# Hybrid decoder layer on one core: other start addresses for the activation tiles, and wide-and-narrow matmul pairs in part of the program

## The chip, the cores and the metric

The kernel runs on one core of one Trainium2 chip. The metric is the device time of one launch, in microseconds (us); the median of three runs of the kernel before is 1642.35 us (1641.98 to 1642.44).

## What is computed

One decoder layer on 256 tokens of width 2048, in float32. An input projection (2048 to 13312 columns) feeds three branches: a gated linear recurrence with 8 heads, causal pooling, and a spatial gating unit. Each branch output of width 1024 is projected to 2048 and weighted by its own gate; the sum goes through an output projection and a layer norm. Then follows a gated feed-forward net with a causal depthwise convolution, and a second layer norm. Cut to what matters here:

```python
merged = (gates[:, :, 0] * (y_hg @ w_hg_proj[l])
          + gates[:, :, 1] * (y_pool @ w_pool_proj[l])
          + gates[:, :, 2] * (y_sg @ w_sg_proj[l]))
mix = merged @ w_out[l]
x = layer_norm(DN_ALPHA * x + mix, ln1_g[l], ln1_b[l])
h = x @ w_up                            # 2048 -> 2 * 5632
acc = conv_b + sum_j conv_w[j] * (h shifted by 2 - j tokens)
a, b = jnp.split(acc, 2, axis=-1)
x = layer_norm(DN_ALPHA * x + (silu(a) * b) @ w_down, ln2_g[l], ln2_b[l])
```

## The kernel before, in words

**Two-part operands.** Every float32 operand of the large products is split (`split`, line 71) into a high part, a rounded copy made by ScalarE, and a low part, the difference made by VectorE. A product is then three matmuls: high x high, high weights x low activations, low weights x high activations. An activation tile holds for each of its k-steps (128 rows of the contraction) 512 columns: 256 tokens of high parts and next to them 256 of low parts.

**Weights.** `pieces` (line 80) loads 1 MB at a time from HBM into `raw` (two buffers), on SP's queue, and splits it into `whi` and `wlo`, a ring of four buffers each, 4 KB a partition and piece. The tiles of `const`, `wst` and the later pools stand one behind the other in each partition; the sizes in front of the ring put every `whi` and `wlo` buffer at 128 modulo 256 bytes, before and after.

**Feature-major groups.** `feat_major` (line 114) computes 256 output features for all 256 tokens: the weights are the stationary operand (128x128) and the activations move, 256 columns at a time. `fm_piece` (line 103) goes k-step by k-step and for each of two column blocks issues the three matmuls of lines 110, 111 and 112, all into the same 256 columns of a PSUM bank. A group over 2048 rows is 16 k-steps, 96 matmuls. The input projection (moving tile X) runs so for its feature-major parts; the branch projections run so with moving tiles y (8 k-steps, 48 matmuls), and the up-projection with x1T. The accumulator tile `mm` (two banks) rotates through three buffers.

**Token-major groups.** `tok_major` (line 138) has the activations as weights and moves 512 columns of `whi` or `wlo`: lines 149 to 151. The value parts of the input projection and the output projection (stationary tile X, for the latter the merged tile that takes X's buffer), and the down-projection (stationary tiles aT).

**Order of the program.** Pool inputs and spatial-gating inputs, the recurrence's inputs, then three merge stages (`merge`, line 601: gate 1, gate 2, gate 0; each 8 times a gate group with X and a projection group with y, with the steps of the recurrence in between), the output projection, the first layer norm, whose transposed result is x1T (`x1T0` and `x1T1`, line 639), the up-projection (line 776: j from 0 to 21, two halves each, so 44 groups; the first has a code of its own, `feat_major_halves`, line 120), and the down-projection. The order on TensorE is as written; on the other engines a scheduler places the work, `hp()` asking for priority. In the up-projection ScalarE and VectorE apply the three taps of the convolution straight from the accumulator into `cv`; only the first group goes through a copy `fm_low` and a sum `h`.

**Where the tiles start.** X is allocated from the right end of the partition, 32768 bytes, and starts at 224 modulo 256. x1T0 and x1T1 come first in the pool `ff` and start at 128; the y tiles in `mix` start at 192; the aT tiles in `up` start at 128.

Of the kernel before, what the change touches and what calls it, by code (L numbers as in the profile page):

```python
# [8 lines left out]
F32 = mybir.dt.float32  # L9
F32R = mybir.dt.float32r  # L10
U8 = mybir.dt.uint8
AF = mybir.ActivationFunctionType
# [4 lines left out]
P = 128  # L17
S = 256
NT = S // P
D = 2048  # L20
KD = D // P
W = 1024
KW = W // P
DFF = 5632
KF = DFF // P
# [4 lines left out]
RMS_EPS = 1e-6  # L30
LEVELS = (64, 32, 16, 8, 4, 2, 1)
RAW_BUFS = 2
KEEP = 14
ENDS = (256, 512)
CROSS = 5
# [5 lines left out]
def hybrid_layer(  # L41
# [6 lines left out]
    nc = tc.nc  # L48
    ctx.enter_context(tc.manual_schedule(engines={ENG.PE}))
    x2 = x[0]  # L50
    win, wup, wout, wdown = w_in[0], w_up[0], w_out[0], w_down[0]

    def hp(level=1):
        return tc.high_priority(offset=1000000 * level)
# [4 lines left out]
    def add(o, a, b):  # L59
        nc.vector.tensor_tensor(out=o, in0=a, in1=b, op=ALU.add)  # L60

    def mul(o, a, b):
        nc.vector.tensor_tensor(out=o, in0=a, in1=b, op=ALU.mult)  # L63

    def stt(o, a, s, b, op0, op1):
        nc.vector.scalar_tensor_tensor(out=o, in0=a, scalar=s, in1=b, op0=op0, op1=op1)  # L66

    def act(o, a, f, **kw):
        nc.scalar.activation(out=o, in_=a, func=f, **kw)  # L69

    def split(hi, lo, src, low=nc.vector):
        act(hi, src, AF.Copy)
        low.tensor_tensor(out=lo, in0=src, in1=hi.bitcast(F32), op=ALU.subtract)  # L73
# [6 lines left out]
    def pieces(w2, col, width, kt_n, big, step, home=None, low=lambda k0: nc.vector):  # L80
        wv = w2.rearrange("(k p) c -> p k c", p=P)
        for b0 in range(0, kt_n, big):
            bn = min(big, kt_n - b0)
            with hp():
                raw = wst.tile([P, bn, width], F32, name="raw", bufs=RAW_BUFS)
                nc.sync.dma_start(out=raw, in_=wv[:, b0:b0 + bn, col:col + width])
            for s0 in range(0, bn, step):
                n = min(step, bn - s0)
                with hp():
                    hi, lo = (home or stage)(b0 + s0, n, width)  # L90
                    split(hi, lo, raw[:, s0:s0 + n, :], low(b0 + s0))
                yield b0 + s0, n, hi, lo

    def stage(k0, n, width):
        return (wst.tile([P, n, width], F32R, name="whi"), wst.tile([P, n, width], F32R, name="wlo"))

    def mm_tile():
        return ps_mm.tile([P, 2, 512], F32, name="mm")
# [1 line left out]
    def ax_tile():  # L100
        return ps_ax.tile([P, 512], F32, name="ax")

    def fm_piece(ps, xT, kt_n, k0, n, hi, lo):
        for k in range(n):
            kt = k0 + k
            for c in range(2):
                cs = slice(c * P, (c + 1) * P)
                xv = xT(kt)
                pc = ps[:, c, 0:S]
                nc.tensor.matmul(pc, lhsT=hi[:, k, cs], rhs=xv[:, 0:S], start=kt == 0, stop=False)  # L110
                nc.tensor.matmul(pc, lhsT=hi[:, k, cs], rhs=xv[:, S:2 * S], start=False, stop=False)  # L111
                nc.tensor.matmul(pc, lhsT=lo[:, k, cs], rhs=xv[:, 0:S], start=False, stop=kt == kt_n - 1)  # L112

    def feat_major(w2, col, xT, kt_n, big=8, step=4, ready=()):
        ps = mm_tile()
        for piece in ready or pieces(w2, col, 256, kt_n, big, step):
            fm_piece(ps, xT, kt_n, *piece)
        return ps[:, :, 0:S]

    def feat_major_halves(kept, xT, kt_n, between):  # L120
        ps = mm_tile()
# [16 lines left out]
    def tok_major(w2, col, xT, kt_n, big=4, step=2, last=0, home=None, done=None, during={}, ends=(512,)):  # L138
# [37 lines left out]
            c0 = c1  # L176
        return ps

    def bc(t, n):
        return t.rearrange("p (a b) -> p a b", b=n)  # L180

# [31 lines left out]

    xpool_cm = tc.tile_pool(name="xpool", bufs=1, side="right", reuse_waits="tile")
    xpool = xpool_cm.__enter__()
    xT_t = xpool.tile([P, KD, 2 * S], F32R, name="X")

    def xT(k):
        return xT_t[:, k, :]

    mix_cm = tc.tile_pool(name="mix", bufs=1, reuse_waits="tile")
    mix = mix_cm.__enter__()
# [10 lines left out]
    def fm_a():  # L233
        return mix.tile([P, 2, S], F32, name="fm_a", bufs=2)
# [11 lines left out]
    def first_block(col):  # L246
# [24 lines left out]
        for i in range(len(STARTS)):  # L271
            cur = nxt
            if i + 1 < len(STARTS):
                nxt = prepare(*STARTS[i + 1])
            else:
                early.extend(next(second) for _ in range(2))
            fm_piece(ps, xT, KD, *cur)
# [84 lines left out]
    for j in range(2):  # L362
        ps = tok_major(win, 6144 + 512 * j, xT, KD)
# [28 lines left out]
    def pool_out(g):  # L392
        ps = feat_major(pool_w[0, g], 0, lambda k: pooled[g][:, k, :], 2, step=2)
        with hp():
            for c in range(2):
                k = 2 * g + c
                scale = pscale[:, k:k + 1]
                hi = y_pool[:, k, 0:S]
                act(hi, ps[:, c, :], AF.Copy, scale=scale)
                stt(y_pool[:, k, S:2 * S], ps[:, c, :], scale, hi.bitcast(F32), ALU.mult, ALU.subtract)  # L400
# [15 lines left out]
    for j in range(4):  # L416
        ps = feat_major(win, 5120 + 256 * j, xT, KD)
# [183 lines left out]
    def merge(first, gi, y, wp, side=()):  # L601
        side = iter(side)
        gcol = 7168 + D * gi
        for j in range(8):
            ps = feat_major(win, gcol + 256 * j, xT, KD)
            gt = fm_a()
            with hp():
                act(gt, ps, AF.Sigmoid)
            next(side, None)
            ps = feat_major(wp, 256 * j, lambda k: y[:, k, :], KW)  # L610
            aj = acc[:, 2 * j:2 * j + 2, :]
            with hp():
                if first:
                    mul(aj, ps, gt)
                else:
                    mul(gt, ps, gt)
                    add(aj, aj, gt)
            next(side, None)
        for _ in side:
            pass  # L620
# [5 lines left out]
    merge(False, 2, y_sg, w_sg_proj[0], hgrn_steps(1, *hgrn(1), o_hg))  # L626
    split(y_hg[:, 4:8, 0:S], y_hg[:, 4:8, S:2 * S], o_hg[1])
    merge(False, 0, y_hg, w_hg_proj[0])
    mT_t = xpool.tile([P, KD, 2 * S], F32R, name="X")
    for j in range(8):  # L630
        split(mT_t[:, 2 * j:2 * j + 2, 0:S], mT_t[:, 2 * j:2 * j + 2, S:2 * S], acc[:, 2 * j:2 * j + 2, :])
    mix_cm.__exit__(None, None, None)
# [3 lines left out]

    ff_cm = tc.tile_pool(name="ff", bufs=1, reuse_waits="tile")
    ff = ff_cm.__enter__()
    x1T_h = [ff.tile([P, KD // 2, 2 * S], F32R, name=f"x1T{i}") for i in range(2)]
    x1 = ff.tile([P, NT, D], F32, name="x1")  # L640
    st1 = ff.tile([P, NT, 4, 6], F32, name="st1")
    for j in range(4):
        cs = slice(512 * j, 512 * (j + 1))
        nc.gpsimd.dma_start(out=x1[:, :, cs], in_=x2[:, cs].rearrange("(t p) c -> p t c", p=P))

    keep_cm = tc.tile_pool(name="keep", bufs=KEEP // 2, reuse_waits="tile")
    keep = keep_cm.__enter__()
# [5 lines left out]
    def keep_home(k0, n, width):  # L653
        if k0 < KD - KEEP:
            return stage(k0, n, width)
        return (keep.tile([P, n, width], F32R, name="khi"), keep.tile([P, n, width], F32R, name="klo"))
# [40 lines left out]
    for j in range(3):  # L697
        cs = slice(512 * j, 512 * (j + 1))
        ps = tok_major(wout, 512 * j, mT, KD)
# [6 lines left out]
    up_next = pieces(wup, DFF, 256, KD, 8, 4)  # L706
    up_early = []
# [26 lines left out]
    def wout_during(c):  # L734
        with hp(2):
            ln1_turn(0, c)
            if 0 < c < 3:
                ln1_low(0, c - 1)
            if c == 2:
                pull()  # L740

    tok_major(wout, 1536, mT, KD, last=KEEP, home=keep_home, done=wout_done,
              during={left: [lambda c=c: wout_during(c)] for c, left in enumerate((5, 3, 2, 0))})
# [29 lines left out]
    up = up_cm.__enter__()  # L773
    aT_t = [up.tile([P, 2, 2 * S], F32R, name=f"aT{j}", bufs=1) for j in range(KF // 2)]

    for j in range(KF // 2):
        ac = []
        for half in range(2):
            if j == 0 and half == 0:
                ps = ps_first  # L780
            else:
                ps = feat_major(wup, half * DFF + 256 * j, x1T, KD, ready=() if j else chain(up_early, up_next))
            if j == 0 and half == 0:
                h = up.tile([P, 2, S], F32, name="h", bufs=1)
                lowp = up.tile([P, 2, S], F32, name="fm_low", bufs=1)
                with hp():
                    for c in range(2):
                        act(lowp[:, c, :], ps[:, c, S:2 * S], AF.Copy)
                        add(h[:, c, :], ps[:, c, 0:S], lowp[:, c, :])
            else:  # L790
                h = ps
            cv = up.tile([P, 2, S], F32, name="cv", bufs=3)
            ac.append(cv)
            with hp():
                for c in range(2):
                    k = half * KF + 2 * j + c
                    act(cv[:, c, :], h[:, c, :], AF.Identity, scale=ccol[:, 2, k:k + 1], bias=ccol[:, 3, k:k + 1])
                    for back in (1, 2):
                        stt(cv[:, c, back:S], h[:, c, 0:S - back], ccol[:, 2 - back, k:k + 1], cv[:, c, back:S],
                            ALU.mult, ALU.add)  # L800
        with hp():
            act(ac[0], ac[0], AF.Silu)
            mul(ac[0], ac[0], ac[1])
            split(aT_t[j][:, :, 0:S], aT_t[j][:, :, S:2 * S], ac[0])
# [59 lines left out]
    for j in range(3):  # L864
        cs = slice(512 * j, 512 * (j + 1))
        ps = tok_major(wdown, 512 * j, aT, KF)
# [50 lines left out]
```

## Time and profile before

| | us |
|---|---|
| median of three runs | 1642.35 |
| profiled execution | 1641.7 |
| its span in the profile | 1640.0 |

The profile is of one execution. "Span" is from its first to its last instruction. TensorE's matmuls overlap, so that a matmul's duration is longer than the distance to the next start; stretches of time with their counts give the pace. PEclk is the granted clock of TensorE as a share of full speed.

### The profile page before, as it was taken

To read this page: it belongs to the slowest core of one execution; us is meant where nothing else is said; L and a number is where in the kernel's file an instruction comes from. 1 tells how busy PE (TensorE), PEld (TensorE's weight loads), DVE (VectorE), ACT (ScalarE), POOL (GpSimd) and SP (SyncE) were. 2 spreads that over 40 slices of the span, in tenths; PEclk is the share of its full clock that TensorE was granted. 3 is DMA by queue.
4 is the path that set the end of the run, shared out by engine and by line. 5 is a ranking of instruction groups with operands and counts; after the bars stand their busy time and mean duration, and the time that the engine had idled before them with its cause. 6 is when DMAs were issued, how large, how long until landed. Compare 5 with 4: busy or idle time off the path is not lost. (4 is left out here: it accounts for less than half of the span.)

```text
span 1640.0 us, 27554 instructions
## 1 busy us (share of the span) xinstructions
PE 1621.4 (99%) x11857; PEld 1542.1 (94%) x11857; DVE 972.0 (59%) x1126; ACT 808.8 (49%) x916; POOL 44.1 (3%) x72
## 2 busy tenths in 40 slices
PE   8999999999999999999999999999999999999997
PEld 8889989999999999999888999999999999888886
DVE  5665447665447765555657665666666665555455
ACT  5454448556458556434444544544554454433332
POOL 1100000000000000000004000000000000000001
PEclk9999999999999999999999999999999999999999
DMA  7755555555555547655563555555555556655553
GB/s 241 229 178 193 180 180 180 181 169 165 181 180 180 180 155 257 205 181 180 184 221 109 180 181 181 183 186 186 188 181 180 181 180 231 205 183 195 194 198 129
DMA packets 254107, 305.59 MB, mean 186 GB/s; under 512 B 5148, under 2 KB 211540, under 8 KB 253472
## 3 DMA queue, kind: packets, MB, share of 16 engines
q1 hardware_dynamic: 251776, 294.67, 55.2%
q0 software_dynamic: 2208, 9.16, 1.7%
q8 instruction: 93, 1.52, 0.4%
q14 instruction: 30, 0.25, 0.0%
HBM read 301.71 MB, written 2.10 MB: 185 GB/s over the span
## 5 line engine op out<-in xcount | busy, mean ns | idle before, releaser
L73 DVE TENSOR_TENSOR wlo<-raw,whi 128x1024 fp32r<-128x1024 f32 x541 | 660.2, 1222 | 573.7 <-ACT whi L69 568.0
L69 ACT ACTIVATE whi<-raw 128x1024 fp32r<-128x1024 f32 x543 | 571.8, 1056 | 741.5 <-PE mm L111 454.2
L110 PE MATMUL mm<-X,whi 128*128 128x256 f32 x1408 | 398.4, 283 | 0.0
L111 PE MATMUL mm<-X,whi 128*128 128x256 f32 x1408 | 397.4, 282 | 0.3 <-DVE X L73 0.3
L112 PE MATMUL mm<-X,wlo 128*128 128x256 f32 x1408 | 396.4, 282 | 0.0
L110 PE MATMUL mm<-x1T,whi 128*128 128x256 f32 x1376 | 389.5, 283 | 0.0
L112 PE MATMUL mm<-x1T,wlo 128*128 128x256 f32 x1376 | 389.4, 283 | 0.0
L111 PE MATMUL mm<-x1T,whi 128*128 128x256 f32 x1376 | 389.4, 283 | 0.0
L112 PEld LDWEIGHTS mm<-X,wlo 128*128 128x128 f32 x1408 | 265.7, 189 | 0.0
L111 PEld LDWEIGHTS mm<-X,whi 128*128 128x128 f32 x1408 | 264.8, 188 | 0.7 <-DVE X L73 0.5
L110 PEld LDWEIGHTS mm<-X,whi 128*128 128x128 f32 x1408 | 265.1, 188 | 0.3
L111 PEld LDWEIGHTS mm<-x1T,whi 128*128 128x128 f32 x1376 | 264.2, 192 | 0.0
L110 PEld LDWEIGHTS mm<-x1T,whi 128*128 128x128 f32 x1376 | 264.2, 192 | 0.0
L112 PEld LDWEIGHTS mm<-x1T,wlo 128*128 128x128 f32 x1376 | 264.2, 192 | 0.0
L149 PE MATMUL mm<-whi,aT 128*128 128x512 f32 (+1 forms) x352 | 135.2, 384 | 0.0
L150 PE MATMUL mm<-wlo,aT 128*128 128x512 f32 (+1 forms) x352 | 135.2, 384 | 0.0
L151 PE MATMUL mm<-whi,aT 128*128 128x512 f32 (+1 forms) x352 | 135.2, 384 | 0.0
L110 PE MATMUL mm<-y,whi 128*128 128x256 f32 x384 | 107.8, 281 | 0.0
L111 PE MATMUL mm<-y,whi 128*128 128x256 f32 x384 | 107.3, 279 | 0.0
L112 PE MATMUL mm<-y,wlo 128*128 128x256 f32 x384 | 107.2, 279 | 0.0
L149 PE MATMUL mm<-whi,X 128*128 128x512 f32 x228 | 90.4, 397 | 0.0
L150 PE MATMUL mm<-wlo,X 128*128 128x512 f32 x228 | 90.4, 396 | 0.0
(188 smaller groups left out, 1521.5 us busy)
## 6 DMA issues: line engine op xcount, KB each, us to landing
raw<-in_w_in_dram SPq DMA_DIRECT2D x102, 1024.0 KB, 5.0
raw<-in_w_up_dram SPq DMA_DIRECT2D x88, 1024.0 KB, 5.1
raw<-in_w_down_dram SPq DMA_DIRECT2D x44, 1024.0 KB, 5.0
raw<-in_w_out_dram SPq DMA_DIRECT2D x16, 1024.0 KB, 5.1
raw<-in_w_pool_proj_dram SPq DMA_DIRECT2D x8, 1024.0 KB, 5.7
raw<-in_w_sg_proj_dram SPq DMA_DIRECT2D x8, 1024.0 KB, 5.7
raw<-in_w_hg_proj_dram SPq DMA_DIRECT2D x8, 1024.0 KB, 5.7
x<-in_x_dram POOLq DMA_DIRECT2D x4, 512.0 KB, 6.8
```

The costliest lines, as they stand in the source:

```text
L69: nc.scalar.activation(out=o, in_=a, func=f, **kw)
L73: low.tensor_tensor(out=lo, in0=src, in1=hi.bitcast(F32), op=ALU.subtract)
L110: nc.tensor.matmul(pc, lhsT=hi[:, k, cs], rhs=xv[:, 0:S], start=kt == 0, stop=False)
L111: nc.tensor.matmul(pc, lhsT=hi[:, k, cs], rhs=xv[:, S:2 * S], start=False, stop=False)
L112: nc.tensor.matmul(pc, lhsT=lo[:, k, cs], rhs=xv[:, 0:S], start=False, stop=kt == kt_n - 1)
L149: nc.tensor.matmul(o[:, w], lhsT=xT(kt)[:, xs], rhs=hi[:, k, w], start=kt == first, stop=False)
L150: nc.tensor.matmul(o[:, w], lhsT=xT(kt)[:, xs], rhs=lo[:, k, w], start=False, stop=False)
L151: nc.tensor.matmul(o[:, w], lhsT=xT(kt)[:, xl], rhs=hi[:, k, w], start=False, stop=kt == kt_n - 1)
```

## The change

Three things are edited.

1. Tiles start elsewhere. X gets 56 words (224 bytes) more, and being allocated from the right it starts at 0 modulo 256 in place of 224. In `ff` 192 bytes are put ahead of x1T, which so starts at 64 in place of 128, and 64 bytes behind `x1`, so that all later tiles keep their residues: aT stays at 128. The y tiles stay at 192. Against the weight ring's 128 that is: X from 96 to 128, x1T from 0 to 192, y 64 and aT 0 as before.
2. `fm_piece` has a second form, `wide`. For a k-step it issues, for each of the two column blocks, one matmul of the high weights with all 512 activation columns (high and low parts side by side, into both halves of a bank), and then for each block the low weights with 256 columns. Four matmuls and four weight loads take the place of six and six.
3. A group in the wide form leaves two partial sums; `whole` copies the right half out on ScalarE and adds it to the left half on VectorE. It is used in the merge stage of gate 2 (8 gate groups) and in the up-projection from j = 11 on (22 groups); the first up-projection group takes its evacuation from it too. `h` and `fm_low` have two buffers.

```diff
-    def fm_piece(ps, xT, kt_n, k0, n, hi, lo):
+    def fm_piece(ps, xT, kt_n, k0, n, hi, lo, wide=False):
         for k in range(n):
             kt = k0 + k
+            if wide:
+                for c in range(2):
+                    nc.tensor.matmul(ps[:, c, :], lhsT=hi[:, k, c * P:(c + 1) * P], rhs=xT(kt)[:, 0:512], start=kt == 0,
+                                     stop=False)
+                for c in range(2):
+                    nc.tensor.matmul(ps[:, c, 0:S], lhsT=lo[:, k, c * P:(c + 1) * P], rhs=xT(kt)[:, 0:S], start=False,
+                                     stop=kt == kt_n - 1)
+                continue
...
-        return ps[:, :, 0:S]
+        return ps if wide else ps[:, :, 0:S]
...
+    def whole(ps, o, lowp):
+        with hp():
+            act(lowp, ps[:, :, S:2 * S], AF.Copy)
+            add(o, ps[:, :, 0:S], lowp)
...
-    xT_t = xpool.tile([P, KD, 2 * S], F32R, name="X")
+    def x_tile():
+        raw = xpool.tile([P, KD * 2 * S + XPAD], F32R, name="X")
+        return raw[:, 0:KD * 2 * S].rearrange("p (k s) -> p k s", s=2 * S)
+
+    xT_t = x_tile()
...
-            ps = feat_major(win, gcol + 256 * j, xT, KD)
+            ps = feat_major(win, gcol + 256 * j, xT, KD, wide=gi == 2)
             gt = fm_a()
+            if gi == 2:
+                whole(ps, gt, mix.tile([P, 2, S], F32, name="fm_low", bufs=2))
+                ps = gt
...
-    mT_t = xpool.tile([P, KD, 2 * S], F32R, name="X")
+    mT_t = x_tile()
...
+    ff.tile([P, 48], F32, name="gap0")
     x1T_h = [ff.tile([P, KD // 2, 2 * S], F32R, name=f"x1T{i}") for i in range(2)]
     x1 = ff.tile([P, NT, D], F32, name="x1")
+    ff.tile([P, 16], F32, name="gap1")
...
-                ps = feat_major(wup, half * DFF + 256 * j, x1T, KD, ready=() if j else chain(up_early, up_next))
-            if j == 0 and half == 0:
-                h = up.tile([P, 2, S], F32, name="h", bufs=1)
-                lowp = up.tile([P, 2, S], F32, name="fm_low", bufs=1)
-                with hp():
-                    for c in range(2):
-                        act(lowp[:, c, :], ps[:, c, S:2 * S], AF.Copy)
-                        add(h[:, c, :], ps[:, c, 0:S], lowp[:, c, :])
+                ps = feat_major(wup, half * DFF + 256 * j, x1T, KD, ready=() if j else chain(up_early, up_next),
+                                wide=j >= KF // 4)
+            if (j == 0 and half == 0) or j >= KF // 4:
+                h = up.tile([P, 2, S], F32, name="h", bufs=2)
+                whole(ps, h, up.tile([P, 2, S], F32, name="fm_low", bufs=2))
             else:
                 h = ps
```

Here XPAD is 56 and KF // 4 is 11. On TensorE, in the up-projection's group j = 11 and the first half, the order before is this (x1T_8138 and x1T_8139 are the two halves of x1T; a k-step is six rows):

```order
L110 MATMUL mm<-x1T_8138,whi 128x256
L111 MATMUL mm<-x1T_8138,whi 128x256
L112 MATMUL mm<-x1T_8138,wlo 128x256
L110 MATMUL mm<-x1T_8138,whi 128x256
L111 MATMUL mm<-x1T_8138,whi 128x256
L112 MATMUL mm<-x1T_8138,wlo 128x256
```

In the changed program the last narrow group (j = 10, second half) ends and the first wide one begins so (x1T_7908 and x1T_7907 are the two halves, the lines those of the changed file):

```order
L119 MATMUL mm<-x1T_7908,whi 128x256
L120 MATMUL mm<-x1T_7908,whi 128x256
L121 MATMUL mm<-x1T_7908,wlo 128x256
L109 MATMUL mm<-x1T_7907,whi 128x512 x2
L112 MATMUL mm<-x1T_7907,wlo 128x256 x2
```

So a k-step is two rows of two: two matmuls of 512 columns, then two of 256.

On VectorE at j = 11, between the multiplication of group j = 10 and that of j = 11, the order before, with what each instruction waits for, is this (`wlo` rows are the weight splits that TensorE lives on; `mm` is the accumulator):

```order
L73 TENSOR_TENSOR wlo<-raw,whi 128x1024 [waits PE_49,Activation_49]
L66 SCALAR_TENSOR_TENSOR cv<-mm,ccol,cv 128x255 [waits Activation_49]
L66 SCALAR_TENSOR_TENSOR cv<-mm,ccol,cv 128x254 [waits DVE_49]
L73 TENSOR_TENSOR wlo<-raw,whi 128x1024 [waits DMAHW4_49,PE_49,Activation_49]
L66 SCALAR_TENSOR_TENSOR cv<-mm,ccol,cv 128x255 [waits Activation_49]
L66 SCALAR_TENSOR_TENSOR cv<-mm,ccol,cv 128x254 [waits DVE_49]
L73 TENSOR_TENSOR wlo<-raw,whi 128x1024 [waits PE_49,Activation_49]
```

And after:

```order
L74 TENSOR_TENSOR wlo<-raw,whi 128x1024 [waits PE_49,Activation_49]
L61 TENSOR_TENSOR h<-mm,fm_low 128x512 [waits Activation_49]
L74 TENSOR_TENSOR wlo<-raw,whi 128x1024 [waits DMAHW4_49,PE_49,Activation_49]
L67 SCALAR_TENSOR_TENSOR cv<-h,ccol,cv 128x255 [waits Activation_49] x2
L67 SCALAR_TENSOR_TENSOR cv<-h,ccol,cv 128x254 [waits DVE_49] x2
L74 TENSOR_TENSOR wlo<-raw,whi 128x1024 [waits PE_49,Activation_49]
```

The add `h` stands in the place of the first convolution steps, the four steps come one split later, and they read `h` and no longer the accumulator.

## Rows read from the trace of the kernel before

**Rows 1.** The page's busy time by engine, and TensorE's granted clock in 40 slices

```profile
PE 1621.4 (99%) x11857; PEld 1542.1 (94%) x11857; DVE 972.0 (59%) x1126; ACT 808.8 (49%) x916; POOL 44.1 (3%) x72
...
PEclk9999999999999999999999999999999999999999
```

**Rows 2.** Waits of TensorE, longest first: total us, times, longest

```profile
PE mm L261 <- DMA t<-in_x_dram: 2.1, 2, 1.7
PE ax L688 <- issue: 1.9, 1, 1.9
PE mm L244 <- DVE cc L201: 1.8, 1, 1.8
```

**Rows 3.** Timeline of TensorE, up-projection: start us, us, engine, line, operands, form

```profile
1000.29 0.28 PE L110 MATMUL mm<-x1T,whi 128*128 128x256 f32 x1
1000.41 0.28 PE L111 MATMUL mm<-x1T,whi 128*128 128x256 f32 x1
1000.53 0.28 PE L112 MATMUL mm<-x1T,wlo 128*128 128x256 f32 x1
```

**Rows 4.** Stretches: X narrow, y, token-major X, x1T narrow, token-major aT

```profile
core 0: us, PE busy (x) PEld busy (x) DVE busy (x) ACT busy (x) POOL busy (x), PEclk, DMA share, GB/s
173.70:208.26 34.56, 34.56 (x290) 34.56 (x289) 14.70 (x12) 15.48 (x16) 0.00 (x0) 1.00 0.57 183
...
724.34:729.99 5.65, 5.65 (x50) 5.65 (x49) 2.45 (x2) 2.60 (x3) 0.00 (x0) 1.00 0.51 159
804.01:848.99 44.98, 44.98 (x193) 36.16 (x192) 25.42 (x25) 17.81 (x17) 0.00 (x0) 1.00 0.61 200
905.98:1378.29 472.31, 472.31 (x3938) 472.31 (x3937) 299.35 (x370) 234.64 (x287) 0.00 (x0) 1.00 0.56 183
1389.81:1509.52 119.71, 119.71 (x530) 99.11 (x529) 59.10 (x54) 47.90 (x47) 0.00 (x0) 1.00 0.62 202
```

**Rows 5.** Timeline of TensorE, a projection group with y: one start and the sixth after it

```profile
725.75 0.28 PE L110 MATMUL mm<-y,whi 128*128 128x256 f32 x1
...
726.46 0.28 PE L110 MATMUL mm<-y,whi 128*128 128x256 f32 x1
```

**Rows 6.** Timeline of TensorE, first up-projection group: a pair, and the sixth pair after it

```profile
880.39 0.33 PE L132 MATMUL mm<-x1T,whi 128*128 128x256 f32 x1
880.57 0.22 PE L134 MATMUL mm<-x1T,wlo 128*128 128x128 f32 x1
...
881.78 0.33 PE L132 MATMUL mm<-x1T,whi 128*128 128x256 f32 x1
```

**Rows 7.** Groups by line and form, ScalarE and VectorE: busy us, mean ns, idle before

```profile
L69 ACT ACTIVATE cv<-mm,ccol 128x256 f32<-128x256 f32 x86 | 47.2, 549 | 0.0
...
L69 ACT ACTIVATE fm_a<-mm 128x512 f32<-128x512 f32 x28 | 16.5, 588 | 0.1
...
L63 DVE TENSOR_TENSOR fm_a<-mm,fm_a 128x512 f32<-128x512 f32 x16 | 11.0, 688 | 4.8 <-PE mm L112 4.8
...
L69 ACT ACTIVATE cv<-h,ccol 128x256 f32<-128x256 f32 x2 | 1.2, 594 | 1.4 <-DVE h L60 1.4
```

**Rows 8.** The page's DMA issues: operands, queue, count, KB each, median us to landing

```profile
raw<-in_w_up_dram SPq DMA_DIRECT2D x88, 1024.0 KB, 5.1
```

More of the change, by code (lines that the diff above doesn't have):

```diff
@@ L32 @@
 RAW_BUFS = 2
+XPAD = 56
 KEEP = 14
@@ L112, in fm_piece, with feat_major @@
                 nc.tensor.matmul(pc, lhsT=lo[:, k, cs], rhs=xv[:, 0:S], start=False, stop=kt == kt_n - 1)
-    def feat_major(w2, col, xT, kt_n, big=8, step=4, ready=()):
+    def feat_major(w2, col, xT, kt_n, big=8, step=4, ready=(), wide=False):
         ps = mm_tile()
         for piece in ready or pieces(w2, col, 256, kt_n, big, step):
-            fm_piece(ps, xT, kt_n, *piece)
-        return ps[:, :, 0:S]
+            fm_piece(ps, xT, kt_n, *piece, wide=wide)
+        return ps if wide else ps[:, :, 0:S]
     def feat_major_halves(kept, xT, kt_n, between):
```

## The prediction

> **What bounds the kernel now.** I read the page first: TensorE is busy for 1621.4 of the 1640.0 us, at a granted clock in the top tenth all along (the 2.4 GHz level); VectorE is busy 59% and ScalarE 49% [rows 1]. So the time is TensorE's. Its waits, summed by what ended them, are a few us in the whole program [rows 2]. Waiting is not what there is to win; the pace of the matmul stream is.
>
> A busy share does not tell a pace, since matmuls overlap: one lasts 0.28 us while the next starts 0.12 us later [rows 3]. So I take stretches that hold whole accumulation groups and divide time by starts [rows 4]; the count has one or two matmuls more than start there, those still running at the left edge.
>
> - X as moving operand, 256 columns: 34.56 us / 288 = 120.0 ns.
> - x1T, 256 columns: 472.31 / 3936 = 120.0 ns, for 41 groups without a break.
> - y (the branch outputs), 256 columns: 5.65 / 48 = 117.7 ns; the single starts agree, 0.71 us for six [rows 5].
> - token-major, 512 columns, X as weights: 44.98 / 192 = 234.3 ns.
> - token-major, 512 columns, aT as weights: 119.71 / 528 = 226.7 ns.
>
> Two readings follow. First, 256 columns more cost 226.7 - 120.0 = 106.7 ns, or 0.417 ns a column; so a matmul carries 120.0 - 106.7 = 13.3 ns whatever its width. Second, equal shapes run at unequal pace. Call the place of an activation tile its start minus that of the weight ring, modulo 256 bytes. From the tile sizes, x1T and aT stand at 0 now, y at 64, X at 96. Place 0 gives 13.3 ns over the columns, place 64 gives 11.0, and X gives 13.3 as moving operand but 234.3 - 213.3 = 21.0 as weights. The clock was the same in all rows [rows 4].
>
> **The change, part by part.** The sum is made against the profiled execution, 1641.7 us; the median of the three runs is 0.65 us above it.
>
> *Pairs in the up-projection.* 22 of the 43 whole groups (j from 11, both halves) take two 512-wide and two 256-wide matmuls in a k-step where six 256-wide ones stood: the same 1536 columns, two fixed costs fewer. At x1T's present place that is 6 x 120.0 = 720.0 against 2 x 226.7 + 2 x 120.0 = 693.4 ns, 26.6 ns less; 22 x 16 = 352 steps give **-9.4 us**.
>
> *Pairs in gate 2.* 8 groups x 16 = 128 steps, again 26.6 ns each: **-3.4 us**. No row has X moving 512 wide. If it took the 234.3 ns of X as weights, a step would save 720.0 - 2 x 234.3 - 2 x 120.0 = 11.4 ns, 1.5 us in all.
>
> *Places.* X goes from 96 to 128, x1T from 0 to 192; y stays at 64 and aT at 0. No row shows 128 or 192. The bounds: at worst a matmul pays what X costs now as weights, 7.6 ns over place 0. At best it runs at the pace of the weight loads alone: in the first up-projection group six pairs of a 256-wide and a 128-wide matmul, 160 ns of columns each, go by in 1.39 us, so 115.8 ns for each of twelve loads [rows 6], 4.2 ns under 120.0. I take y's row, 2.3 ns less, since it is nearest: 64, 128 and 192 are all whole steps of 64 and none is 0, whereas 96, which gains nothing, is no such step. The Trainium skill's page "SBUF — State Buffer", section "Who interferes with whom", says that TensorE reads its moving operand and its weights through two independent ports and never waits on anyone; by that a place would be worth nothing and this term zero. The trace does not agree: 117.7 against 120.0 ns for one shape at one clock [rows 4].
> With it go 3456 narrow matmuls of X (1152 k-and-column steps x 3), 2016 of x1T (672 x 3), and the 1920 of the pairs: 7392 x 2.3 = **-17.0 us**.
>
> *Token-major with X.* 768 matmuls hold X or the merged tile, which takes its buffer, as weights. From 234.3 to aT's 226.7 is 7.6 ns, 5.8 us; with y's 2.3 on top 9.9 ns: **-7.6 us**. At worst it stays 234.3, no gain.
>
> *Evacuation.* Each of the 30 paired groups adds a ScalarE copy of 128x512 out of PSUM and a VectorE add, by the rows of such shapes 588 and 688 ns [rows 7]; cv then reads h, 594 against 549 ns, twice. I cost this at nothing. In the 41 up groups VectorE is busy 299.35 and ScalarE 234.64 of 472.31 us [rows 4], 7.3 and 5.7 us a group; with the new work 8.0 and 6.4 us of a group that shrinks to some 10.9 us. In the queue the add stands between two weight subtractions, as the convolution steps did, and waits for the copy; behind it wait weight pieces, of which the ring holds four, 2.7 us of TensorE's work each. The accumulators rotate through three, so one is wanted back two groups, over 20 us, later. Without that cover it is 30 x 1.28 = 38 us. The joined evacuation of the first group (one copy and one add for two of each) and the 36 last matmuls that read a spare tile at a new place come to under 0.1 us.
>
> *Loads.* 1 MB serves 8 k-steps, 5.76 us now and about 5.5 us in pairs, and takes 5.1 us to land [rows 8], with two buffers. The last stage already takes 1 MB per 24 x 226.7 ns = 5.44 us with TensorE busy throughout [rows 4]. So nothing here.
>
> Sum: 9.4 + 3.4 + 17.0 + 7.6 = 37.4 us; 1641.7 - 37.4 = 1604.3, and 0.65 for the median: **1605 us**.
>
> **The rivals.**
> A. *Places are worth nothing*, and y's pace has another cause, say the buffers that lie around it. For it: one row alone is faster, and X at 96, not at 0 either, runs at 120.0. Against: y and X alternate in one stage through one ring, and 234.3 against 226.7 again goes with the place. Then only pairs count, 9.4 + 3.4 = 12.8 us: 1629.5; if X moving 512 wide is slow, 1631.5; if X gains as weights alone, 1623.7. The rule on ports of the Trainium skill's page "SBUF — State Buffer", section "Who interferes with whom", leads here too.
> B. *The new places are better than y's*, and the weight loads' 115.8 ns is the limit: 7392 x 4.2 = 31.0, and 768 x (234.3 - 222.5) = 9.1: 12.8 + 31.0 + 9.1 = 52.9, so 1589.5. For it: nothing says that 64 is the best. Against: y's rows have the same loads and don't reach it.
> C. *The new places are bad*, slower than before: 128 or 192 costs each matmul what X's place costs in the token-major rows. 7392 x 7.6 = 56.2 us, less the pairs' 12.8: 1685.7. It decides from 12.8 us / 7392 = 1.7 ns a matmul. For it: places do cost, and two of the values were never seen. Against: the one bad row is the one off the steps of 64.
> D. *The evacuation is not covered*: the 38 us come back and the change moves nothing, about 1643. Against it stand the loads worked out above.
>
> **How the numbers follow.** Forecast 0.52, A 0.26, B 0.12, C 0.07, D 0.03. Runs differ by under 0.03%, but 0.2% (3.3 us) is about what a measurement can tell from no change. Forecast, A and B are faster, 0.90; D the same, 0.03; C slower, 0.07. The range takes the forecast and A to its upper bound (1631.5); these hold 0.78, so it also reaches down to B's end, 1590.
>
> **What would show it.** In the profile after, stretches of whole groups: x1T narrow at 117.7 ns a matmul (A: 120.0; B: towards 115.8; C: 127.6), a paired k-step at 2 x 224.4 + 2 x 117.7 = 684 ns, so 10.95 us a group (A: 693 ns), X narrow at 117.7, token-major with X at 224.4, and y and aT as before at 117.7 and 226.7. D shows as TensorE waiting for whi or wlo in the second half of the up-projection. The prediction is wrong if x1T narrow stays at 120.0, or if X and x1T differ: then 128 and 192 are not alike, which I assume.

## The result, and the profile after

The changed kernel takes 1618.87 us (median of three runs, 1617.99 to 1620.2) where the kernel before took 1642.35: ratio 0.9859, 95% interval 0.9836 to 0.9881. It is faster by 23.5 us (1.4%), inside the range, and 14 us slower than the forecast's 1605. Its profiled execution took 1620.2 us with a span of 1618.5, 21.5 us under the span before.

TensorE is as busy as before [rows 1], and its waits are the same few, at the start and the layer norm [rows 2]. The page's busy time by engine, after:

```profile
PE 1599.2 (99%) x10897; PEld 1479.5 (91%) x10897; DVE 985.2 (61%) x1155; ACT 825.9 (51%) x945; POOL 44.3 (3%) x72
```

So again the paces tell it. The stretches after, in the view of [rows 4]: X narrow, a paired group of gate 2, y, token-major with X, x1T narrow, x1T paired, token-major with aT.

```profile
core 0: us, PE busy (x) PEld busy (x) DVE busy (x) ACT busy (x) POOL busy (x), PEclk, DMA share, GB/s
173.55:207.72 34.17, 34.17 (x290) 34.17 (x289) 14.71 (x12) 15.47 (x16) 0.00 (x0) 1.00 0.58 184
491.72:502.90 11.18, 11.18 (x66) 9.78 (x65) 6.72 (x9) 11.00 (x12) 0.00 (x0) 1.00 0.57 186
734.51:740.16 5.65, 5.65 (x50) 5.65 (x49) 2.45 (x2) 2.61 (x3) 0.00 (x0) 1.00 0.54 156
796.65:841.45 44.80, 44.80 (x193) 36.04 (x192) 25.41 (x25) 17.82 (x17) 0.00 (x0) 1.00 0.61 200
898.13:1124.27 226.14, 226.14 (x1923) 226.14 (x1921) 145.57 (x180) 114.52 (x140) 0.00 (x0) 1.00 0.58 189
1124.27:1368.33 244.06, 244.06 (x1410) 214.11 (x1409) 168.32 (x219) 138.06 (x176) 1.12 (x2) 1.00 0.59 193
1368.33:1488.03 119.70, 119.70 (x531) 99.11 (x530) 59.55 (x55) 48.43 (x48) 0.00 (x0) 1.00 0.61 202
```

Divided by what starts in each (288, 64, 48, 192, 1920, 1408 and 528 matmuls):

| stretch | place before, after | before | forecast | after |
|---|---|---|---|---|
| X narrow, ns a matmul | 96, 128 | 120.0 | 117.7 | 118.6 |
| x1T narrow | 0, 192 | 120.0 | 117.7 | 117.8 |
| y narrow | 64, 64 | 117.7 | 117.7 | 117.7 |
| token-major, X as weights | 96, 128 | 234.3 | 224.4 | 233.3 |
| token-major, aT as weights | 0, 0 | 226.7 | 226.7 | 226.7 |
| paired k-step with x1T, ns | 0, 192 | 720.0 | 684 | 693.4 |
| paired k-step with X | 96, 128 | 720.0 | 684 | 699 |

The y row is of one group out of 24; not all of them run at this pace, as the section on the prediction shows. The narrow stage of x1T came out as forecast. The 512-wide matmuls, as pairs and with X as weights, did not: the first part of the loss is there.

### The profile page after: what moved, and what is told of

Same layout as the page of the kernel before. It is cut to its first block, busy times and chain, and to the rows that moved or that the text cites. A ratio compares the mean times of both kernels' runs of the same rounds, so it can differ in the third digit from the quotient of the medians.

```text
span 1618.5 us, 25700 instructions
## 1 busy us (share of the span) xinstructions
PE 1599.2 (99%) x10897; PEld 1479.5 (91%) x10897; DVE 985.2 (61%) x1155; ACT 825.9 (51%) x945; POOL 44.3 (3%) x72
## 5 line engine op out<-in xcount | busy, mean ns | idle before, releaser
L119 PE MATMUL mm<-X,whi 128*128 128x256 f32 x1152 | 326.4, 283 | 0.0
L121 PE MATMUL mm<-X,wlo 128*128 128x256 f32 x1152 | 325.2, 282 | 0.0
L120 PE MATMUL mm<-X,whi 128*128 128x256 f32 x1152 | 325.1, 282 | 0.1
L109 PE MATMUL mm<-x1T,whi 128*128 128x512 f32 x704 | 219.6, 393 | 0.0
L120 PEld LDWEIGHTS mm<-X,whi 128*128 128x128 f32 x1152 | 217.9, 189 | 0.5 <-DVE X L74 0.3
L119 PEld LDWEIGHTS mm<-X,whi 128*128 128x128 f32 x1152 | 217.9, 189 | 0.2
L121 PEld LDWEIGHTS mm<-X,wlo 128*128 128x128 f32 x1152 | 217.6, 189 | 0.0
L119 PE MATMUL mm<-x1T,whi 128*128 128x256 f32 x672 | 188.9, 281 | 0.0
L120 PE MATMUL mm<-x1T,whi 128*128 128x256 f32 x672 | 188.8, 281 | 0.0
L121 PE MATMUL mm<-x1T,wlo 128*128 128x256 f32 x672 | 188.8, 281 | 0.0
L112 PEld LDWEIGHTS mm<-x1T,wlo 128*128 128x128 f32 x704 | 132.4, 188 | 30.0
L112 PE MATMUL mm<-x1T,wlo 128*128 128x256 f32 x704 | 138.8, 278 | 0.0
L119 PEld LDWEIGHTS mm<-x1T,whi 128*128 128x128 f32 x672 | 129.0, 192 | 0.0
L120 PEld LDWEIGHTS mm<-x1T,whi 128*128 128x128 f32 x672 | 126.1, 188 | 0.0
L121 PEld LDWEIGHTS mm<-x1T,wlo 128*128 128x128 f32 x672 | 126.1, 188 | 0.0
L119 PE MATMUL mm<-y,whi 128*128 128x256 f32 x384 | 107.7, 281 | 0.0
```

The source lines that it names most:

```text
L109: nc.tensor.matmul(ps[:, c, :], lhsT=hi[:, k, c * P:(c + 1) * P], rhs=xT(kt)[:, 0:512], start=kt == 0, stop=False)
L112: nc.tensor.matmul(ps[:, c, 0:S], lhsT=lo[:, k, c * P:(c + 1) * P], rhs=xT(kt)[:, 0:S], start=False, stop=kt == kt_n - 1)
```

## The experiments

Places are given as in the prediction, start of the activation tile minus start of the weight ring, modulo 256 bytes. Where a run was timed, the kernel before ran on the same chip beside it (medians 1641.04, 1642.44 and 1642.76 us in the three sessions).

**A scan of the places.** To separate the place from the tile, one kernel reads the same tile from other places.

```diff
+        off = place // 4
...
+            flat = x1T_h[kt // 8].rearrange("p k s -> p (k s)")
+            b = 2 * S * (kt % 8) + off
...
+                    nc.tensor.matmul(pc, lhsT=hi[:, k, cs], rhs=flat[:, b:b + S], start=kt == 0, stop=False)
+                    nc.tensor.matmul(pc, lhsT=hi[:, k, cs], rhs=flat[:, b + 192:b + 192 + S], start=False, stop=False)
+                    nc.tensor.matmul(pc, lhsT=lo[:, k, cs], rhs=flat[:, b:b + S], start=False, stop=last)
```

The second matmul's columns begin 192 words (768 bytes, three times 256) behind those of the first, so that all three stand at the same place; in the other kernels it is 1024 bytes, four times 256.

> The kernel before, with the start of the activation operand shifted inside its tile: each whole group of the up-projection reads x1T from another place (start minus weight ring, modulo 256 bytes, in steps of 16), first 16 groups in the 256-wide form, then 16 in the paired form, then 7 and 4 again in another order; the three whole down-projection groups take their weights from aT at 16 places, 8 k-steps each. The shifted operands hold other columns, so the sums are not the reference's. Theory by form: pace follows the place alone, each form in its own way: 256-wide 120.0 ns at place 0, 117.8 at 64 and 192, 118.7 at 128, about 120.0 at 96; the paired step 693 ns at 0 and at 192, about 698 at 128; token-major 226.7 ns at place 0 and 232 to 234 at 96 and 128. Theory by tile: pace belongs to the tile and its stage, so every group of x1T runs at 120.0 ns whatever its place, every paired step alike, and every stretch of aT at 226.7 ns.

Stretches of TensorE, first 256-wide groups of 96 matmuls at places 0, 64, 96, 112, 128, 192, 192 again (another group ahead of it) and 8, then paired groups of 64 at 0, 64, 128 and 192:

```profile
core 0: us, PE busy (x), PEclk, DMA share, GB/s
893.44:905.01 11.57, 11.57 (x98) 1.00 0.73 229
938.97:950.28 11.31, 11.31 (x99) 1.00 0.58 185
961.80:973.32 11.52, 11.52 (x99) 1.00 0.57 185
973.32:984.20 10.88, 10.88 (x99) 1.00 0.55 179
984.20:995.58 11.38, 11.38 (x98) 1.00 0.61 196
1029.69:1040.58 10.89, 10.89 (x99) 1.00 0.57 183
1253.72:1264.62 10.90, 10.90 (x99) 1.00 0.56 183
1310.34:1322.47 12.13, 12.13 (x98) 1.00 0.56 183
1074.63:1085.77 11.14, 11.14 (x66) 1.00 0.58 190
1119.23:1130.29 11.06, 11.06 (x66) 1.00 0.55 186
1164.03:1175.19 11.16, 11.16 (x66) 1.00 0.58 191
1208.88:1219.98 11.10, 11.10 (x66) 1.00 0.57 186
```

And token-major stretches of 48 matmuls with aT as weights at places 0, 112, 128, 192 and 240:

```profile
1378.58:1389.46 10.88, 10.88 (x50) 1.00 0.69 258
1456.30:1467.49 11.19, 11.19 (x49) 1.00 0.59 190
1467.49:1478.70 11.21, 11.21 (x50) 1.00 0.57 187
1512.13:1523.12 10.99, 10.99 (x50) 1.00 0.61 189
1545.51:1556.41 10.90, 10.90 (x49) 1.00 0.57 184
```

The whole scan, worked out in the same way from the trace (narrow: ns a matmul; pairs: ns a k-step; token-major: ns a matmul):

| place | 0 | 16 | 32 | 48 | 64 | 80 | 96 | 112 | 128 | 144 | 160 | 176 | 192 | 208 | 224 | 240 |
|---|---|---|---|---|---|---|---|---|---|---|---|---|---|---|---|---|
| narrow | 120.0 | 118.8 | 116.7 | 118.3 | 117.8 | 120.0 | 120.0 | **113.3** | 118.6 | 118.7 | 117.3 | 119.3 | **113.4** | 119.2 | 118.3 | 117.2 |
| pairs | 696 | 698 | 694 | 700 | **692** | 704 | 707 | 698 | 698 | 695 | 703 | 707 | 694 | 709 | 702 | 698 |
| token-major | **226.9** | **226.8** | 233.3 | 233.3 | 233.2 | 231.8 | 234.1 | 233.2 | 233.4 | 233.4 | 233.2 | 229.9 | 229.0 | 233.2 | 233.3 | **227.1** |

(Place 0's first group, 120.5 as a whole, has one longer start; its second half and its repetition run at 120.0 and 119.9, and 120.0 is entered.) One tile in one stage runs at 113.3 to 120.0 ns by its place alone, and off the steps of 16 at 126.4 (place 8) and 120.9 (place 72). So the pace goes with the place: the theory by tile falls. And each form goes its own way: a token-major matmul is fastest at 0, 16 and 240, where the narrow one is slow or middling. The pairs in the scan have no evacuation of the second half, and still take 694 ns at 192, as in the changed kernel (693.4): the evacuation costs the pairs nothing. One number was not expected by any theory: 113.4 ns at place 192, where the changed kernel runs at 117.8.

**The places alone.**

```diff
-            ps = feat_major(win, gcol + 256 * j, xT, KD, wide=gi == 2)
+            ps = feat_major(win, gcol + 256 * j, xT, KD)
...
-                ps = feat_major(wup, half * DFF + 256 * j, x1T, KD, ready=() if j else chain(up_early, up_next),
-                                wide=j >= KF // 4)
+                ps = feat_major(wup, half * DFF + 256 * j, x1T, KD, ready=() if j else chain(up_early, up_next))
```

> The change without its pairs: all groups 256-wide, tiles at the new places. By the paces of the changed kernel (x1T 117.8, X 118.7, token-major X 233.3): 43 x1T groups x 0.21 us, 44 X groups x 0.12 us and 16 token-major groups x 0.09 us, 15.8 us less than before: about 1626.5 us. By the forecast's step (2.3 ns from every matmul and 9.9 ns from the token-major ones): 8352 x 2.3 + 7.6 = 26.8 us less, 1615.5 us.

Median 1624.74 us, ratio 0.9872 (0.9821 to 0.9924): 16.3 us less than the 1641.04 beside it. By the paces of the changed kernel, x1T's 43 groups give 4128 x 2.2 ns = 9.1 us, X's some 5 and token-major 0.8: about 15, where the forecast's step gave more. But the four runs are 1625.57, 1624.63, 1606.59 and 1624.84: one is 18 us faster. The profile is of the first; x1T there is at 117.8 ns (42 groups, 4032 matmuls):

```profile
898.78:1373.66 474.88, 474.88 (x4035) 1.00 0.58 190
```

With 113.3 in place of 117.8 ns, 43 groups would take 43 x 96 x 4.4 = 18.2 us less. That fits the odd run and the scan's place 192: one place, two paces. The odd run itself has no profile, so its pace is inferred from its time.

**The pairs alone.** XPAD is 0 and the two gaps in `ff` are left out; the rest as in the change.

> The change without its places: X at 96, x1T at 0, the same pairs. Theory by form: the paired step of x1T at 693 ns as at place 192, 9.4 us less; gate 2 with X at 96 somewhere between 693 and 709 ns a step, 1.5 to 3.4 us less: 1629.5 to 1631.5 us. If the new places had given their 2.3 ns to the 512-wide matmuls and the evacuation took it back, the step at place 0 would carry the evacuation's loss too, about 9 ns over 693, and the time were about 1634 us.

1631.23 us, ratio 0.9939 (0.9924 to 0.9954): 9.8 us less. The paired stretch of x1T at place 0, 22 groups of 64 matmuls:

```profile
1134.44:1379.67 245.23, 245.23 (x1410) 1.00 0.59 193
```

That is 245.23 us / 352 = 696.7 ns a k-step, as in the scan, 23.3 ns under six narrow ones; the forecast had 693.4 from the token-major rows. Gate 2 with X at 96 is at 703 ns in its steady groups (175.8 ns x 64 / 16). So the pairs' own gain is about 8.2 + 2.2 us of the 12.8 forecast. A loss to the evacuation, which would have put the step at some 702 ns here, is not there.

**X at place 0.** XPAD is 24 in place of 56; all else as in the change.

> The change with X at place 0 in place of 128. Theory by form: X narrow 120.0 ns (4.6 us more over 3456), token-major with X 226.7 ns (5.1 us less over 768), a paired step with X 693 ns (0.6 us less): about 1 us less than the changed kernel, some 1618 us, with the paces as the proof. Theory by tile: X keeps 118.7 and 233.3 ns, or goes back to 120.0 and 234.3.

1619.09 us, the changed kernel's time within the runs' spread (1618.44 to 1621.12), where 1618 was expected; the time cannot tell 1 us. The profile can: a token-major stretch of 96 matmuls and a narrow group of 96:

```profile
205.83:227.62 21.79, 21.79 (x99) 1.00 0.57 188
637.65:649.17 11.52, 11.52 (x98) 1.00 0.84 297
```

227.0 ns as weights where X took 233.3, and 120.0 ns as the moving tile where it took 118.6. One address serves two forms that want different ones, and by these paces the two nearly cancel (768 x 6.3 = 4.8 us less, 3168 x 1.4 = 4.4 us more).

**All at place 112.** No pairs, and X, x1T and y begin so many bytes inside somewhat longer tiles that each stands at 112.

```diff
+    def placed(pool, n, name, off, **kw):
+        raw = pool.tile([P, n * 2 * S + XPAD], F32R, name=name, **kw)
+        return raw[:, off:off + n * 2 * S].rearrange("p (k s) -> p k s", s=2 * S)
...
-    xT_t = x_tile()
+    xT_t = placed(xpool, KD, "X", 4)
```

> No pairs; X, x1T and y all at place 112, where the scan ran at 113.3 ns a 256-wide matmul. If the scan's pace holds for a whole stage: 4224 matmuls of X and 4128 of x1T x 6.7 ns, 1152 of y x 4.5 ns, 768 token-major ones x 1 ns: 61.6 us less than before, about 1580 us. Rival: the 113.3 ns is one of two paces that a stage can fall into, as at place 192 (117.8 in the changed kernel, 113.3 in the scan); then some stages run at 117 to 120 ns and the time lies anywhere between 1580 and 1640 us.

1589.61 us, ratio 0.9678 (0.9664 to 0.9693). The 42 groups of x1T behind the first whole one (4032 matmuls):

```profile
881.00:1337.96 456.96, 456.96 (x4034) 1.00 0.60 197
```

That is 113.3 ns a matmul (the first group 114.4, with its longer start). X in its undisturbed groups is at 113.3 to 113.8, y at 113.3, and token-major with X at 233.6. The rival, a stage that falls into a slower pace, did not come. The missing 9 us are a new wait, which the run after next takes up.

**One paired group ahead of the narrow ones.** The places of the change, and only the first whole group of the up-projection in pairs. Against the run with the places alone:

```diff
-                ps = feat_major(wup, half * DFF + 256 * j, x1T, KD, ready=() if j else chain(up_early, up_next))
-            if j == 0 and half == 0:
+                ps = feat_major(wup, half * DFF + 256 * j, x1T, KD, ready=() if j else chain(up_early, up_next),
+                                wide=j == 0)
+            if j == 0:
```

> Places of the change, no pairs but one: the first whole group of the up-projection is paired, the 42 behind it are 256-wide at place 192. In the scan a group at 192 ran at 113.3 ns behind a group of another pattern, twice; in the changed kernel and in the run with places alone at 117.8. Theory that the pattern ahead sets the pace: 113.3 ns in all 42 groups in every run, 42 x 96 x 4.4 = 17.9 us under the run with places alone, about 1606.5 us. Rival, that the pace is drawn anew in each run whatever stands ahead: 1624.5 us in most runs and 1606.5 in a few.

1607.70 us, all four runs between 1606.77 and 1608.44. The paired group, and the 42 narrow groups behind it:

```profile
887.74:898.90 11.16, 11.16 (x66) 1.00 0.66 215
898.90:1355.86 456.96, 456.96 (x4034) 1.00 0.59 197
```

456.96 / 4032 = 113.3 ns, against 117.8 for the same matmuls from the same place without that group (474.88 us above). So at this place what goes ahead decides which of its two paces the stage then keeps for 450 us. The rival, a draw anew in each run, had most runs at 1624.5; none of the four was there, and it is out for this order. Without the paired group one run of four came out 18 us faster, so that order does not fix the pace in every run.

**The merged tile at place 0.** As the run at place 112, with `mT_t` at 0.

```diff
-    mT_t = placed(xpool, KD, "X", 4)
+    mT_t = placed(xpool, KD, "X", 40)
```

> As the run with all at place 112, and the merged tile, which serves as weights in the output projection, at place 0. By form: its 384 token-major matmuls go from 233.2 to 226.7 ns, 2.5 us less than that run; the same time if pace belonged to the stage.

1588.75 us, 0.9 us under the run at 112 where 2.5 were expected. The three whole output-projection groups did go from 233.3 to 226.7 ns, but the new wait was longer in this profile (4.9 against 3.8 us at its head), so of the size only the pace is shown. The waits of TensorE and then of ScalarE in this run (total, times, longest), and the stretch that they stand in:

```profile
PE mm L119 <- ACT whi L70: 4.9, 1, 4.9
```

```profile
ACT whi L70 <- DMA raw<-in_w_hg_proj_dram: 13.6, 1, 13.6
```

```profile
core 0: us, PE busy (x) PEld busy (x) DVE busy (x) ACT busy (x) POOL busy (x), PEclk, DMA share, GB/s
620.00:640.00 20.00, 14.54 (x109) 14.05 (x109) 7.13 (x8) 4.96 (x6) 0.00 (x0) 0.88 0.80 293
640.00:660.00 20.00, 20.00 (x169) 20.00 (x168) 9.44 (x10) 7.92 (x8) 0.00 (x0) 0.95 0.62 201
```

TensorE idles 5.5 us, and behind the idle time its granted clock falls to half, the 1.2 GHz level, from about 636 to 642 us (0.88 and 0.95 of full speed over the stretches above). TensorE alone there:

```profile
636.00:642.00 6.00, 5.52 (x26) 0.50 0.59 190
```

A piece of weights, issued at 616.7 us, lands 17.3 us later, where such a piece otherwise takes some 5 to 6 us; meanwhile the DMA engines move 293 GB/s. On POOL's queue the residual input `x` and the two vectors `gb` were issued just before:

```profile
613.83 2.94 POOL L662 DMA_DIRECT2D x<-in_x_dram  x4 [504.68 <-DVE t L67]
616.77 0.57 POOL L668 DMA_DIRECT2D gb<-in_ln_g_dram  x1
617.33 0.54 POOL L669 DMA_DIRECT2D gb<-in_ln_b_dram  x1
```

**Those loads one by one.** As the last run; a column of gate stage 0's sum is copied to a spare word, and each quarter of the residual input waits for one.

```diff
+            if gi == 0 and j % 2 == 0:
+                act(cc[:, 4 + j // 2:5 + j // 2], aj[:, 0, 0:1], AF.Copy)
...
+            nc.gpsimd.tensor_copy(out=x1[:, 0, 512 * j:512 * j + 1], in_=cc[:, 4 + j:5 + j])
+            nc.gpsimd.dma_start(out=x1[:, :, cs], in_=x2[:, cs].rearrange("(t p) c -> p t c", p=P))
```

> As the run with all at place 112 and the merged tile at 0, whose TensorE stood still some 9 us around 616 to 640 us, where POOL's queue loads the residual input (2 MB) and two vectors spread over the partitions (2 MB). Here each quarter of the residual input waits for a sum of gate stage 0, so the loads come one by one some 33 us apart, and the two vectors last. If those loads took the DMA engines from the weights: the 9 us come back, about 1580 us. If the weights were late for another reason (splits queued behind the work between the two stages): 1588 us as before.

1580.17 us (1579.72 to 1580.52), ratio 0.9622 (0.9607 to 0.9636). The same stretch now:

```profile
620.00:640.00 20.00, 20.00 (x179) 20.00 (x178) 11.66 (x11) 8.13 (x9) 1.66 (x2) 1.00 0.59 186
640.00:660.00 20.00, 20.00 (x179) 20.00 (x178) 9.87 (x9) 8.59 (x9) 0.00 (x0) 1.00 0.65 217
```

No idle time, the clock at 1.00, and 8.6 of the expected 9 us are back. So the loads on POOL's queue had made the weights late. This is the fastest version found: 62.6 us under the kernel before, 39 us under the changed one, with no pair in it.

**The pairs first.** The change with the two halves of the up-projection exchanged (`wide=j < KF // 4`).

> The change with its two halves of the up-projection exchanged: the paired groups first (j below 11), the 256-wide ones behind them; the same instructions in number. If the pattern ahead sets the pace at place 192: the 22 groups from j = 11 at 113.3 in place of 117.8 ns, 22 x 96 x 4.4 = 9.3 us under the changed kernel, about 1609.5 us (paired steps 693 ns as before). If not: 1619 us.

1610.26 us, ratio 0.9803 (0.9787 to 0.982), 8.6 us under the changed kernel. The 21 paired groups and the 22 narrow ones:

```profile
886.43:1119.46 233.03, 233.03 (x1347) 1.00 0.58 193
1119.46:1358.82 239.36, 239.36 (x2115) 1.00 0.59 197
```

The narrow ones run at 239.36 / 2112 = 113.3 ns, 680 ns a k-step, and the pairs at 693.5. So the same instructions in another order are worth 9 us, and beside the faster of this place's two paces the pairs are the slower form.

## Why the prediction was right in its sign and range, and where it went wrong

What bounds the kernel, the covered evacuation and the covered loads held, and so did the number for the narrow stage of x1T, in part by luck, as shown below. The time lies in the range, but nearer to the lowest value of rival A (1623.7) than to the forecast: the paired step came out at A's 693 ns and not at 684. Summed by the paces of the profile after, against the terms of the forecast:

| term | forecast, us | measured, us |
|---|---|---|
| pairs in the up-projection, with their place | 9.4 + 3.2 | 352 x 26.6 = 9.4 |
| pairs in gate 2, with their place | 3.4 + 1.2 | 128 x 21 = 2.7 |
| X narrow | 7.9 | 3168 x 1.4 = 4.4 |
| x1T narrow | 4.6 | 2016 x 2.2 = 4.4 |
| token-major with X | 7.6 | 768 x 1.0 = 0.8 |
| sum | 37.3 | 21.7 |

(The place term of 17.0 us is divided by its 3456, 2016, 1408 and 512 matmuls; of X's narrow ones 288 stay at 120.0 ns after, see below.) The profiled spans differ by 21.5 us. Not in the table are 1.1 us from y, which gained without being moved (see below), and 0.9 us by which the first matmuls with X start later after (20.16 against 19.26 us).

The step that failed is the one named *Places* and its use in *Token-major with X*: "I take y's row, 2.3 ns less, since it is nearest: 64, 128 and 192 are all whole steps of 64", applied to matmuls of either width and to tiles as weights. The row was of 256-wide matmuls with the activation moving. For 512-wide ones the scan shows something else: as weights a tile at 128 takes 233.4 ns, no better than the 234.3 that X had at 96, while place 0 gives 226.7, which the forecast had taken for a middle value to be improved on. That is 6.8 us of the 15.6 that are missing. The pairs, half 512-wide, have a little less gain of their own than the token-major rows said (10.4 of 12.8 us, the run of the pairs alone), and their places gave little on top of it: 696.7 ns a k-step at 0, 693.4 at 192. Together that is 5.1 us less than forecast, gate 2 included. And 128 is not 64: X narrow came to 118.6, 3.5 us short. The prediction had named this sign: it is wrong "if X and x1T differ", and they do, 118.6 against 117.8.

A second step is weaker than it looked: the 13.3 ns that a matmul carries "whatever its width". At place 0 it nearly holds, since the pairs save 23.3 of the 26.6 ns a k-step. At 112 six narrow matmuls take 6 x 113.3 = 680 ns and the pairs 698 in the scan, and at 192 the numbers are 680 and 693.5: two matmuls fewer save nothing there. What a pair saves depends on the place too.

Rival A, places worth nothing, is out: one tile gave 113.3 to 120.0 ns by its place in one stage, and in the scan each place tried twice came out within 0.6 ns of itself. The Trainium skill's page "SBUF — State Buffer", section "Who interferes with whom", from which that rival also followed, has TensorE's two reads on independent ports and the engine waiting on no one; the scan's row of 16 places does not agree. Rival C's price was real for other matmuls than it had in mind: a place can cost some 7 ns, but here only the 512-wide form with the activation as weights pays it at 128 (233.4 against 226.9 at 0), and the narrow form pays 6.4 at 8, a place that the change does not use. Rival B's price was too modest: 115.8 ns from the pairs of the first group was no lower bound, since 113.3 is reached at 112 and 192. D is out: the pairs run as fast with the evacuation (693.4 ns) as without (694).

What the prediction missed is that one place can have two paces. The trace before had a sign of it. The prediction reads y's pace from one group, 117.7 ns [rows 4], and says against rival B that y's rows don't reach 115.8. One of the 24 y groups before does (TensorE alone):

```profile
542.09:547.53 5.44, 5.44 (x49) 1.00 0.51 150
```

That is 5.44 / 48 = 113.3 ns, from the same place 64. In the profile after, six of the 24 run so behind a longer first start, though y was not moved. The second half of one of them, 24 matmuls:

```profile
340.45:343.17 2.72, 2.72 (x26) 1.00 0.84 245
```

Again 113.3 ns. Five more such groups than before are the 1.1 us of y named above (5 x 48 x 4.4 ns). Which groups are fast repeats: the same ones in the profiles of the changed kernel and of the pairs-first run, whose programs are alike up to there, and the same ones in the runs with the places alone and with one paired group. So the program decides here, but not by the matmuls just ahead alone, since fast and slow y groups of the changed kernel follow the same ones.

X shows it, too. In the changed kernel X at 128 runs three narrow groups at 118.6 ns ahead of the token-major group of the branch inputs (207.7 to 230.0 us), and three behind it at 120.0. The stretches of TensorE alone (us, PE busy, granted clock, DMA share, GB/s):

```profile
173.55:207.72 34.17, 34.17 (x290) 1.00 0.58 184
230.04:264.60 34.56, 34.56 (x289) 1.00 0.55 179
```

Both are 288 matmuls of the same shape from the same tile: 34.17 / 288 = 118.6 ns and 34.56 / 288 = 120.0. At 192 the two paces are 117.8 and 113.3, and the change happened to order its groups so that x1T's stage falls into the slower one. That x1T narrow came out at the forecast's 117.7 was therefore luck: with a paired group ahead the same place gives 113.3, and no row before spoke of 192.

## What to carry to other kernels

Where TensorE is busy throughout, divide stretches of the trace by their starts, per form and tile, before counting instructions: a few ns a matmul on ten thousand of them were 62 us here. Read more than one group of each, since equal groups can differ. Don't carry a pace from one form to another; scan the start addresses of the moving and the stationary tile against the weight ring in one kernel, each form by itself, and try the order of the stages too, since a stage can keep a slow pace that another beginning avoids. Then look for the load that the faster stream now runs into.

## What the runs showed of the hardware that was not expected

- The pace of one and the same 256-wide float32r matmul goes from 113.3 (place 112) to 126.4 ns (place 8) with the start of the moving tile alone, at a granted clock of 1.00 throughout; the order is not smooth in the place.
- 512-wide matmuls with the activation as weights take 226.7 to 227.1 ns at places 0, 16 and 240, some 233 to 234 at most others, and 229 to 232 at 80, 176 and 192.
- Two matmuls fewer are not always a gain: at 112 and 192, where the narrow form reaches 113.3 ns, a k-step of six narrow matmuls takes 680 ns and of four in pairs 698 and 693.5.
- At place 192 the narrow stage keeps, over 42 groups, the pace with which it begins: 117.8 ns behind the first up-projection group (by the times, in three runs of four), 113.3 behind a paired one (in four of four). At place 64 y's groups run at 117.7 or 113.3 ns. What puts a stage into one pace or the other, and why it keeps it, is not settled. No run tried places beyond 256 bytes or moved the weight ring alone, so what the two reads share is open too.
